# FFN gate and up by Strassen's method: seven quadrant products for eight, weight sums formed by accumulating DMAs

## The chip, the cores and the metric

One Trainium2 chip, one of its cores. The metric is the device time of one launch in microseconds (us); the kernel before takes 1047.01 us, the median of three runs (1046.59 to 1047.04). The rows and numbers of the trace come from one profiled execution with a span of 1045.3 us.

## What is computed

One decoder layer for 512 tokens, d_model 1024, float32: a half-step SwiGLU FFN, a mixing stage (a gated linear recurrence and a latent attention with a common input and output projection), a second half-step FFN, a per-layer embedding with a gate, and a final norm. The FFN, which the change is about, is

```python
def swiglu(x, w_gate, w_up, w_down):
    return (jax.nn.silu(x @ w_gate) * (x @ w_up)) @ w_down

h = h + 0.5 * swiglu(rms_norm(h, ln_ffn1[i]), w1_gate[i], w1_up[i], w1_down[i])   # D_FF = 2816
...
h = h + 0.5 * swiglu(rms_norm(h, ln_ffn2[i]), w2_gate[i], w2_up[i], w2_down[i])
```

## The kernel before

The residual `h` lies in SBUF as eight tiles of 128 features by 512 tokens (features on the partitions). All weights come from HBM as one stream of 128x128 blocks in the order of their use. `WStream.load` (L49) brings 16 blocks (1 MB) by one DMA of the SP queue into one of three raw tiles; `_split` (L68) turns eight blocks at a time into two float32r parts, `whi` by ScalarE (L70, a rounding copy) and `wlo` by VectorE (L71, raw minus high part). Of each part there are three tiles, and the splits run up to three pieces ahead of TensorE (`W.ahead`). Activations are split in the same way: `Norm.add` (L223) makes `xh` and `xl` of gain times `h` (L169, L170), and adds up the squares for the norm (L238, L239). The row factor of the norm, `rb`, is multiplied on after the product.

One block product is `mm3` (L157 to L161): three float32r matmuls, high by high, high by low, low by high, each of 128x128 stationary weights by 512 moving columns. Each matmul record has a weight-load record beside it.

`ffn` (L255) runs over 22 blocks of 128 hidden features. For each it makes the gate and the up product (`gu`, eight `mm3` each, one PSUM bank each, from the pools `acc` and `t` of three banks), and then the chain of L277 to L285: gate times `rb` (VectorE), Silu (ScalarE), times up (VectorE), and the split of the result into `ah` and `al`. After all 22 the `down` product runs (L291 to L298): eight blocks of 128 output features, 22 `mm3` each, times 0.5 and `rb`, added to `h`, and `next_norm.add`. In the first FFN three of the first products are taken k by k while `x` still arrives; after the fourth block `make_tables` (L302) makes the cosine and sine tables on VectorE, with two small DMAs of the POOL queue (L305, L336). In the output projection (L744 to L749) `n2.add` prepares the second FFN's input.

Within an engine the instructions stand in the order that a compile-time list scheduler chose: of the ready ones, the one that comes first in the program. So an engine is rarely held up by a waiting instruction that stands first in the text, but work that stands earlier in the text goes first wherever it is ready.

Of the kernel before, what the change touches and what calls it, by code (L numbers as in the profile page):

```python
# [29 lines left out]
RAW = 16  # L30

# columns of the packed vectors
# [5 lines left out]
class WStream:  # L38
    """The weights as one stream of 128x128 blocks in the order of their use, each split
    exactly into two float32r parts."""  # L40

    def __init__(self, nc, pool, dram, loads):
        self.nc, self.pool, self.dram = nc, pool, dram
        self.loads = list(loads)
        self.raws, self.ready, self.left = [], [], []
        self.n_load = self.n_piece = 0
        self.ahead = 1

    def load(self):  # L49
        start, n = self.loads.pop(0)  # L50
        t = self.pool.tile([P, RAW * P], F32, tag="wraw", name=f"wraw{self.n_load}", bufs=3)
        self.n_load += 1
        src = self.dram[start * P * P:(start + n) * P * P].rearrange("(p c) -> p c", p=P)
        self.nc.sync.dma_start(t[:, :n * P], src)
        self.raws += [(t, o, min(CH, n - o)) for o in range(0, n, CH)]

    def _piece(self):
        if not self.raws:
            self.load()
        raw, o, n = self.raws.pop(0)  # L60
        c = self.n_piece
        self.n_piece += 1
        hi = self.pool.tile([P, CH * P], F32R, tag="whi", name=f"whi{c}", bufs=3)
        lo = self.pool.tile([P, CH * P], F32R, tag="wlo", name=f"wlo{c}", bufs=3)
        self._split(raw, o, n, hi, lo)
        self.ready.append([(hi, lo, o, n) for o in range(n)])

    def _split(self, raw, o, n, hi, lo):  # L68
        src = raw[:, o * P:(o + n) * P]
        self.nc.scalar.activation(hi[:, :n * P], src, AF.Copy)  # L70
        self.nc.vector.tensor_tensor(lo[:, :n * P], src, hi[:, :n * P].bitcast(F32), op=ALU.subtract)  # L71

    def keep(self, new):
        """The next half of a piece in tiles of its own."""
        if not self.raws:
            self.load()
        raw, o, n = self.raws.pop(0)
        n_now = CH // 2
        if n > n_now:
            self.raws.insert(0, (raw, o + n_now, n - n_now))  # L80
        hi, lo = new("kh", F32R), new("kl", F32R)
        self._split(raw, o, n_now, hi, lo)
        return hi, lo

    def next(self, n=1):
        if not self.left:
            while len(self.ready) < self.ahead and (self.raws or self.loads):
                self._piece()
            self.left = self.ready.pop(0)
# [5 lines left out]


@with_exitstack
def block_kernel(ctx: ExitStack, tc: tile.TileContext, xT, pT, pos, wst, loads, vecs, lnf, cmask, tmask, out):
# [8 lines left out]
    W = WStream(nc, wpool, wst, loads)  # L107
# [27 lines left out]
    for k in range(KD):  # L135
        nc.sync.dma_start(h[k], xT[k * P:(k + 1) * P, :])
        if k < 4:
            W.load()
# [14 lines left out]

    def vcol(c):
# [8 lines left out]
    def split(src, hi, lo, g=None):  # L163
        """hi + lo = src * g, exactly."""
# [7 lines left out]
    def rsqrt_of(ss, n, width):  # L172
        """1 / sqrt(ss / width + eps) of a [P, n] view, by Newton's iteration."""
# [21 lines left out]
    def col_sums(sqs, out):  # L195
        """out[:, j] = sums over partitions (and over the tiles) of token block j."""
# [5 lines left out]
    def broadcast_ps(r):  # L202
        """[P tokens, 4 blocks] -> the same row of 512 tokens on every partition, in PSUM."""
# [13 lines left out]
    class Norm:  # L217
        """Splits g * h tile by tile, and gathers the sum of squares."""

        def __init__(self, gcol):  # L220
            self.gcol, self.hi, self.lo, self.sum = gcol, [], [], None

        def add(self, k, square=True):  # L223
            hi = tmp.tile([P, T], F32R, tag=f"xh{k}", name=nm("xh"), bufs=1)
            lo = tmp.tile([P, T], F32R, tag=f"xl{k}", name=nm("xl"), bufs=1)
            split(h[k], hi, lo, vcol(self.gcol + k))
            self.hi.append(hi)
            self.lo.append(lo)
# [11 lines left out]

        def finish(self):
# [6 lines left out]

    def row_bcast(r, tag):
# [5 lines left out]
    def ffn(norm, next_norm, first=(), extra=None):  # L255
        a_hi, a_lo = [], []
        first = list(first)

        def product(new):
            if first:  # L260
                return first.pop(0)
            u = new("gu")
            for k in range(KD):
                mm3(u, W.next(), norm.x(k), k == 0, k == KD - 1)
            return u

        waiting = []
        for f in range(KF):
            waiting.append((product(acc), product(tps)))
            if f == 0:  # L270
                r = norm.finish()
                continue
            if f == 1:
                rb = row_bcast(r, "rb")
            for g, u in waiting:
                gs = tmpt("gs")
                V.tensor_tensor(gs, g, rb, op=ALU.mult)  # L277
# [568 lines left out]
def _blocks(w1_gate, w1_up, w1_down, w_in, w_q_up, w_kv_up, w_out, w2_gate, w2_up, w2_down, w_ple_gate, w_ple_proj):  # L846
# [7 lines left out]
    def col(n):  # L854
        return slice(n, n + P)
# [92 lines left out]
```

## Time and profile before

| | |
|---|---|
| median of three runs | 1047.01 us |
| span of the profiled execution | 1045.3 us |
| TensorE busy in the span | 1034.2 us (99%), 4763 matmuls |
| VectorE / ScalarE busy | 519.2 us (50%) / 356.8 us (34%) |
| DMA | 97.48 MB, mean 93 GB/s |
| share of gate and up in the chain that ended last | 3 lines of 15% each |
| share of down in it | 3 lines of 8% each |

The page counts a matmul as busy from its start to its modelled end (389 ns here), and matmuls overlap; what one costs is read from the distance of the starts in the timeline. In a group of instructions the columns are: line, engine, operation, names and shapes, count | busy us, mean ns of one | idle time before them and what ended it.

### The profile page before, as it was taken

What the parts mean: (1) busy time and instruction counts of PE and PEld (TensorE: products, weight loads), DVE (VectorE), ACT (ScalarE), POOL (GpSimd) and SP (SyncE); (2) the same over time, 40 slices, a digit from 0 to 9 for tenths busy, and PEclk for the clock granted to TensorE, in tenths of its full rate; (3) what the DMA queues carried; (4) which work ended last, traced back from release to release, by engine and by line L of the source; (5) the groups of instructions that cost most, each with busy time, mean ns of one, the idle gap of its engine ahead of it and who ended that gap; (6) DMA issues with size and microseconds to landing.
All of it is one profiled execution on the core that took longest, in us unless ns stands there. A gap on an engine that the chain in (4) does not pass through costs nothing.

```text
span 1045.3 us, 11742 instructions
## 1 busy us (share of the span) xinstructions
PE 1034.2 (99%) x4763; PEld 845.5 (81%) x4763; DVE 519.2 (50%) x929; ACT 356.8 (34%) x567; POOL 2.5 (0%) x9
## 2 busy tenths in 40 slices
PE   9999999999999999999999999999999999999996
PEld 7888888888888888887666788888888888888885
DVE  7574433443343368775647655334443343344555
ACT  7333322233222232345444434322333232223332
POOL 0000000000000000000000000000000000000000
PEclk9999999999999999999999999999999999999998
DMA  7322323223232231212210232232232322323301
GB/s 285 116 102 82 119 81 109 93 84 118 81 104 98 83 119 42 71 61 91 91 41 1 81 103 98 81 114 88 85 117 80 118 84 87 116 81 126 116 22 60
DMA packets 16726, 97.48 MB, mean 93 GB/s; under 512 B 2096, under 2 KB 2352, under 8 KB 6048
## 3 DMA queue, kind: packets, MB, share of 16 engines
q1 hardware_dynamic: 16512, 96.24, 26.5%
q8 instruction: 37, 0.61, 0.2%
q0 software_dynamic: 160, 0.49, 0.2%
q14 instruction: 17, 0.14, 0.0%
HBM read 94.10 MB, written 2.10 MB: 92 GB/s over the span
## 4 chain that ended last, share of the span: by engine, by line
PE 97%; DMA 1%; DVE 1%; ACT 1%; issue 0%; SPq 0%; ACTq 0%; DVEq 0%
PE gu L160 15%; PE gu L159 15%; PE gu L161 15%; PE down L160 8%; PE down L159 8%; PE down L161 8%; PE ufq L159 2%; PE wo L159 1%; PE ufq L161 1%; PE ufq L160 1%; PE wo L160 1%; PE wo L161 1%; PE pg L159 1%; PE pg L161 1%; PE pg L160 1%; PE sl L536 1%
## 5 line engine op out<-in xcount | busy, mean ns | idle before, releaser
L70 ACT ACTIVATE whi<-wraw 128x1024 fp32r<-128x1024 f32 (+2 forms) x168 | 176.0, 1047 | 526.3 <-PE gu L160 187.2
L71 DVE TENSOR_TENSOR wlo<-wraw,whi 128x1024 fp32r<-128x1024 f32 (+2 forms) x168 | 203.0, 1208 | 150.0 <-ACT whi L70 148.4
L159 PE MATMUL gu<-xh,whi 128*128 128x512 f32 x704 | 274.4, 390 | 0.0
L161 PE MATMUL gu<-xh,wlo 128*128 128x512 f32 x704 | 274.0, 389 | 0.2 <-DVE wlo L71 0.2
L160 PE MATMUL gu<-xl,whi 128*128 128x512 f32 x704 | 273.8, 389 | 0.0
L159 PEld LDWEIGHTS gu<-xh,whi 128*128 128x128 f32 x704 | 132.3, 188 | 28.5 <-ACT whi L70 1.1
L161 PEld LDWEIGHTS gu<-xh,wlo 128*128 128x128 f32 x704 | 132.2, 188 | 28.1 <-DVE wlo L71 0.9
L160 PEld LDWEIGHTS gu<-xl,whi 128*128 128x128 f32 x704 | 132.2, 188 | 27.5
L159 PE MATMUL down<-ah,whi 128*128 128x512 f32 x352 | 136.9, 389 | 0.0
L160 PE MATMUL down<-al,whi 128*128 128x512 f32 x352 | 136.9, 389 | 0.0
L161 PE MATMUL down<-ah,wlo 128*128 128x512 f32 x352 | 136.9, 389 | 0.0
L282 DVE TENSOR_TENSOR a<-gu,gs 128x512 f32<-128x512 f32 x44 | 30.4, 691 | 128.3 <-PE gu L161 126.9
L277 DVE TENSOR_TENSOR gs<-gu,rb 128x512 f32<-128x512 f32 x44 | 30.3, 690 | 97.5 <-PE gu L161 97.3
L159 PEld LDWEIGHTS down<-ah,whi 128*128 128x128 f32 x352 | 66.1, 188 | 13.8
L161 PEld LDWEIGHTS down<-ah,wlo 128*128 128x128 f32 x352 | 66.1, 188 | 13.7
L160 PEld LDWEIGHTS down<-al,whi 128*128 128x128 f32 x352 | 66.1, 188 | 13.6
L169 ACT ACTIVATE xh<-h,vec 128x512 fp32r<-128x512 f32 x32 | 22.8, 718 | 27.9 <-DVE h L297 25.9
L167 DVE TENSOR_TENSOR al<-a,ah 128x512 fp32r<-128x512 f32 x44 | 30.1, 685 | 1.1 <-ACT ah L166 0.7
L166 ACT ACTIVATE ah<-a 128x512 fp32r<-128x512 f32 x44 | 27.8, 633 | 5.8 <-DVE a L282 5.8
L170 DVE SCALAR_TENSOR_TENSOR xl<-h,vec,xh 128x512 fp32r<-128x512 f32 x32 | 23.7, 747 | 9.5 <-ACT xh L169 9.5
L278 ACT ACTIVATE gs<-gs 128x512 f32<-128x512 f32 x44 | 27.2, 617 | 0.3
L159 PE MATMUL ufq<-xh,whi 128*128 128x512 f32 x64 | 26.2, 410 | 0.0
(256 smaller groups left out, 1092.7 us busy)
## 6 DMA issues: line engine op xcount, KB each, us to landing
wraw<-wst SPq DMA_DIRECT2D x83, 1024.0 KB, 4.9
h<-xT SPq DMA_DIRECT2D x8, 256.0 KB, 4.9
out<-y SPq DMA_DIRECT2D x8, 256.0 KB, 2.3
wraw<-wst SPq DMA_DIRECT2D x3, 384.0 KB, 5.4
wraw<-wst SPq DMA_DIRECT2D x2, 512.0 KB, 3.8
wraw<-wst SPq DMA_DIRECT2D x1, 768.0 KB, 4.2
rpb<-rpa SPq DMA_DIRECT2D x8, 64.0 KB, 2.0
praw<-pT SPq DMA_DIRECT2D x2, 256.0 KB, 4.0
```

The lines of the kernel that those rows point to most:

```text
L70: self.nc.scalar.activation(hi[:, :n * P], src, AF.Copy)
L71: self.nc.vector.tensor_tensor(lo[:, :n * P], src, hi[:, :n * P].bitcast(F32), op=ALU.subtract)
L159: PE.matmul(out, a[0], b[0], start=start, stop=False)
L160: PE.matmul(out, a[0], b[1], start=False, stop=False)
L161: PE.matmul(out, a[1], b[0], start=False, stop=stop)
L166: S.activation(hi, src, AF.Copy)
L167: V.tensor_tensor(lo, src, hi.bitcast(F32), op=ALU.subtract)
L169: S.activation(hi, src, AF.Copy, scale=g)
L170: V.scalar_tensor_tensor(lo, src, g, hi.bitcast(F32), op0=ALU.mult, op1=ALU.subtract)
L277: V.tensor_tensor(gs, g, rb, op=ALU.mult)
L278: S.activation(gs, gs, AF.Silu)
L282: V.tensor_tensor(a, u, gs, op=ALU.mult)
```

## The change

The gate and up products of hidden blocks 2 to 21 are made in ten pairs of blocks by Strassen's method in Winograd's form. The input is cut in four quadrants (two halves of 256 tokens by two halves of 512 features: A11, A12, A21, A22), the weights of a pair in four too (gate and up by two halves of the rows: B11, B12, B21, B22, eight 128x128 blocks each). Seven products of quadrants or sums of them take the place of eight: A11 B11, A12 B21, S1 T1, S2 T2, S3 T3, S4 B22, A22 T4. Each is 2 x 4 x 3 matmuls of 256 moving columns. Blocks 0 and 1 are still made in the old way.

- The sums S1 to S4 of the input are made once per FFN on VectorE and split (`Norm.forms`): in the first FFN after the input's splits, in the second within the output projection.
- The sums T1 to T4 of the weights are made in raw tiles: B12 is loaded, negated twice by ScalarE into the tiles N and Q, and DMAs of the POOL queue add quadrants from HBM onto them (`_add`): N + B11 is T1, then N + B22 is T2, Q + B22 is T3, and after one more negation by ScalarE N + B21 is T4, up to signs. All seven weight operands of a pair are split as before.
- Partial results are read from PSUM in between by ScalarE and VectorE (`start_pair`, `end_pair`), the next pair's first two products stand between this pair's.
- `down` runs in two halves: over blocks 0 to 11 after the fifth pair, over 12 to 21 at the end; both add to `h`.
- Loads are 8 blocks (0.5 MB) now, into seven raw tiles; the scratch space for descriptors shrinks to 2048 bytes. The first FFN starts with four products k by k, not three.

```diff
-RAW = 16
+NRAW = 7
+HT = T // 2
+MO = [0, 4, 1, 5, 2, 6, 3, 7]
...
+    def load(self, start, n):
+        t = self.raw()
+        self.nc.sync.dma_start(t[:, :n * P], self.source(start, n))
+        return t
...
+    def _add(self, t, g, name):
+        self.nc.gpsimd.dma_start(out=t, in_=self.source(GROUPS[g][name], CH), accum_op=ALU.add)
+
+    def _begin(self, g):
+        if g not in GROUPS or g in self.groups:
+            return
+        S = self.nc.scalar
+        d = self.groups[g] = {"N": self.load(GROUPS[g]["B12"], CH), "Q": self.raw()}
+        S.activation(d["Q"], d["N"], AF.Copy, scale=-1.0)
+        S.activation(d["N"], d["N"], AF.Copy, scale=-1.0)
+        self._add(d["N"], g, "B11")
+        self._add(d["Q"], g, "B22")
+
+    def _form(self, g, what):
+        self._begin(g)
+        d = self.groups[g]
+        if what in ("T1", "T2", "T4"):
+            return d["N"]
+        return d["Q"] if what == "T3" else self.load(GROUPS[g][what], CH)
+
+    def _formed(self, g, what):
+        d = self.groups[g]
+        if what == "T1":
+            self._add(d["N"], g, "B22")
+        elif what == "B11":
+            self._begin(g + 1)
+        elif what == "T3":
+            self.nc.scalar.activation(d["N"], d["N"], AF.Copy, scale=-1.0)
+            self._add(d["N"], g, "B21")
...
+        def forms(self, k):
+            left, right = slice(0, HT), slice(HT, T)
+            c, c2 = self.gcol + k, self.gcol + k + 4
+            a21 = tmpt("a21", tag="sq", bufs=2)[:, :HT]
+            f = tmp.tile([P, 4, HT], F32, tag="at", name=nm("sf"), bufs=1)
+            S.activation(a21, h[k][:, right], AF.Copy, scale=vcol(c))
+            V.scalar_tensor_tensor(f[:, 0], h[k + 4][:, right], vneg[:, c2:c2 + 1], a21, op0=ALU.mult, op1=ALU.subtract)
+            V.scalar_tensor_tensor(f[:, 1], h[k][:, left], vneg[:, c:c + 1], f[:, 0], op0=ALU.mult, op1=ALU.subtract)
+            V.scalar_tensor_tensor(f[:, 2], h[k][:, left], vcol(c), a21, op0=ALU.mult, op1=ALU.subtract)
+            V.scalar_tensor_tensor(f[:, 3], h[k + 4][:, left], vcol(c2), f[:, 1], op0=ALU.mult, op1=ALU.subtract)
+            for i in range(4):
+                t = slot("sx", F32R).rearrange("p (two t) -> p two t", two=2)
+                split(f[:, i], t[:, 0], t[:, 1])
+                self.s[k, i + 1] = t
...
+        def product(bank, what, begin=False, end=False):
+            hi, lo = W.form()
+            for i in range(2):
+                o = bank[:, i * HT:(i + 1) * HT]
+                for k in range(4):
+                    c = slice((2 * k + i) * P, (2 * k + i + 1) * P)
+                    x = norm.operand(what, k)
+                    PE.matmul(o, hi[:, c], x[:, 0], start=begin and i == 0 and k == 0, stop=False, skip_group_check=True)
+                    PE.matmul(o, hi[:, c], x[:, 1], start=False, stop=False, skip_group_check=True)
+                    PE.matmul(o, lo[:, c], x[:, 0], start=False, stop=end and i == 1 and k == 3, skip_group_check=True)
...
+        def start_pair(d):
+            d["c"] = tps("c")
+            product(d["c"], "S1", begin=True)
+            yield
+            d["a"] = acc("a")
+            product(d["a"], "A11", begin=True)
+            d["m1"] = tmpt("m1")
+            S.activation(d["m1"], d["a"], AF.Copy)
+            yield
+
+        def end_pair(f, d, between):
+            b = tps("b")
+            product(b, "A12", begin=True, end=True)
+            gs1 = tmpt("gs")
+            V.tensor_tensor(gs1, b, d["m1"], op=ALU.add)
+            V.tensor_tensor(by_half(gs1), by_half(gs1), r_of(0), op=ALU.mult)
+            S.activation(gs1, gs1, AF.Silu)
+            product(d["a"], "S2")
+            u2 = slot("u2")
+            S.activation(u2, d["a"], AF.Copy)
+            next(between, None)
+            product(d["a"], "S3")
+            u3 = slot("u3")
+            S.activation(u3, d["a"], AF.Copy)
+            V.tensor_tensor(u3, d["c"], u3, op=ALU.add)
+            next(between, None)
+            product(d["c"], "S4", end=True)
+            V.tensor_tensor(u2, d["c"], u2, op=ALU.add)
+            product(d["a"], "A22", end=True)
+            at = tmp.tile([P, 2, T], F32, tag="at", name=nm("at"), bufs=1)
+            V.tensor_tensor(at[:, 0], u2, gs1, op=ALU.mult)
+            gs2 = tmpt("gs")
+            V.tensor_tensor(by_half(gs2), by_half(d["a"]), r_of(1), op=ALU.mult)
+            S.activation(gs2, gs2, AF.Silu)
+            V.tensor_tensor(at[:, 1], u3, gs2, op=ALU.mult)
+            for i in range(2):
+                gated(f + i, at[:, :, i * HT:(i + 1) * HT])
...
+        second = down(range(12, KF), True)
+        for f in range(2, KF, 2):
+            d_next = {}
+            end_pair(f, d, start_pair(d_next) if f + 2 < KF else second)
+            d = d_next
+            if f == 10:
+                for _ in down(range(12), False):
+                    pass
+        for _ in second:
+            pass
...
-    first = [acc("gu"), tps("gu"), acc("gu")]
-    for k in range(KD):
+    first = [acc("gu"), tps("gu"), acc("gu"), tps("gu")]
+    for k in MO:
         n1.add(k, square=False)
         for u in first:
-            mm3(u, W.next(), n1.x(k), k == 0, k == KD - 1)
+            mm3(u, W.next(), n1.x(k), k == MO[0], k == MO[-1])
+    for k in range(4):
+        n1.forms(k)
...
+        for p in range(PAIRS):
+            forms(p, "B21", "T2")
+            forms(p + 1, "T1")
...
+            forms(p, "T3")
+            forms(p + 1, "B11")
...
+            forms(p, "B22", "T4")
+            if p == 4:
+                down(range(12))
```

## Rows read from the trace of the kernel before

**Rows 1.** The page: its head, the engines' busy time, the chain's shares by engine.
```profile
span 1045.3 us, 11742 instructions
PE 1034.2 (99%) x4763; PEld 845.5 (81%) x4763; DVE 519.2 (50%) x929; ACT 356.8 (34%) x567; POOL 2.5 (0%) x9
...
PE 97%; DMA 1%; DVE 1%; ACT 1%; issue 0%; SPq 0%; ACTq 0%; DVEq 0%
```

**Rows 2.** Timeline, gate and up, 30 matmuls apart: start us, us, engine, line, tile.
```profile
643.44 0.39 PE L161 MATMUL gu<-xh,wlo 128*128 128x512 f32 x1
...
650.24 0.39 PE L161 MATMUL gu<-xh,wlo 128*128 128x512 f32 x1
```

**Rows 3.** Timeline, mixing stage: 448 columns (12 apart) and 512 columns (10 apart).
```profile
440.15 0.36 PE L161 MATMUL uc<-whi,xl 128*128 128x448 f32 x1
...
442.59 0.36 PE L161 MATMUL uc<-whi,xl 128*128 128x448 f32 x1
...
394.25 0.39 PE L159 MATMUL ufq<-xh,whi 128*128 128x512 f32 x1
...
396.55 0.39 PE L160 MATMUL ufq<-xl,whi 128*128 128x512 f32 x1
```

**Rows 4.** Chain of work in order of time: start us, us, piece; plain float32 matmuls.
```profile
498.58 0.43 PE sc L569 x2
...
545.70 2.23 PE oh L715 x20
```

**Rows 5.** Groups by line, shapes apart: VectorE and ScalarE instructions.
```profile
L71 DVE TENSOR_TENSOR wlo<-wraw,whi 128x1024 fp32r<-128x1024 f32 x162 | 198.3, 1224 | 149.5 <-ACT whi L70 147.9
L282 DVE TENSOR_TENSOR a<-gu,gs 128x512 f32<-128x512 f32 x44 | 30.4, 691 | 128.3 <-PE gu L161 126.9 <-ACT gs L278 1.4
L170 DVE SCALAR_TENSOR_TENSOR xl<-h,vec,xh 128x512 fp32r<-128x512 f32 x32 | 23.7, 747 | 9.5 <-ACT xh L169 9.5
L405 DVE TENSOR_TENSOR qe<-ufq,rb 128x256 f32<-128x256 f32 x8 | 3.1, 416 | 5.3 <-PE ufq L161 5.3
L70 ACT ACTIVATE whi<-wraw 128x1024 fp32r<-128x1024 f32 x162 | 171.8, 1060 | 525.2 <-PE gu L160 187.2 <-issue 151.0 <-PE down L160 126.6
L166 ACT ACTIVATE ah<-a 128x512 fp32r<-128x512 f32 x44 | 27.8, 633 | 5.8 <-DVE a L282 5.8
L252 ACT ACTIVATE rb<-rbp 128x512 f32<-128x512 f32 x3 | 1.7, 580 | 0.0
```

**Rows 6.** Windows: stretch, us, busy us of the engines, clock, DMA share, GB/s.
```profile
0.00:25.00 25.00, 23.27 (x92) 17.68 (x93) 17.52 (x34) 18.93 (x29) 1.38 (x7) 1.00 0.82 298
...
100.00:200.00 100.00, 100.00 (x443) 82.80 (x442) 40.60 (x46) 29.59 (x37) 0.00 (x0) 1.00 0.27 95
...
570.00:628.00 58.00, 57.98 (x267) 47.00 (x265) 33.20 (x47) 24.06 (x37) 0.00 (x0) 1.00 0.26 89
```

**Rows 7.** DMA issues: size of one, median us from issue to landing.
```profile
wraw<-wst SPq DMA_DIRECT2D x83, 1024.0 KB, 4.9
...
wraw<-wst SPq DMA_DIRECT2D x2, 512.0 KB, 3.8
...
posi<-pos POOLq DMA_DIRECT2D x1, 256.0 KB, 3.7
```

**Rows 8.** Timeline of the first FFN: VectorE's and TensorE's start, the tables on VectorE.
```profile
4.87 0.75 DVE L170 SCALAR_TENSOR_TENSOR xl<-h,vec,xh 128x512 fp32r<-128x512 f32 x1 [1.86 <-ACT xh L169]
...
5.30 0.97 PE L159 MATMUL gu<-xh,whi 128*128 128x512 f32 x2
...
54.99 0.42 DVE L307 CAST ang<-posi 128x512 f32<-128x512 int32 x1
...
64.02 0.42 DVE L326 TENSOR_SCALAR kr<-kr 128x512 f32<-128x512 f32 x1
```

More of the change, by code (lines that the diff above doesn't have):

```diff
@@ L52, in load, with raw, source @@
+    def raw(self):
+        t = self.pool.tile([P, CH * P], F32, tag="wraw", name=f"wraw{self.n_load}", bufs=NRAW)
         self.n_load += 1
[L53 to L60, printed above, removed]
+        return t
+    def source(self, start, n):
+        return self.dram[start * P * P:(start + n) * P * P].rearrange("(p c) -> p c", p=P)
@@ L62, in _piece @@
         self.n_piece += 1
[L63 to L71, printed above, removed]
@@ L73, in keep, with _plain @@
-    def keep(self, new):
[L75 to L80, printed above, removed]
+        return (self.pool.tile([P, CH * P], F32R, tag="whi", name=f"whi{c}", bufs=3),
+                self.pool.tile([P, CH * P], F32R, tag="wlo", name=f"wlo{c}", bufs=3))
+    def _plain(self, start, n):
+        t = self.raws.pop(0) if self.raws else self.load(start, n)
+        hi, lo = self._pair()
+        self._split(t[:, :n * P], hi[:, :n * P], lo[:, :n * P])
+        return [(hi, lo, o, n) for o in range(n)]
@@ new lines, in _piece @@
+    def _piece(self):
+        kind, x, n = self.items.pop(0)
+        if kind == "p":
+            self.ready.append(self._plain(x, n))
+        else:
+            t = self._form(x, n)
+            hi, lo = self._pair()
+            self._split(t, hi, lo)
+            self._formed(x, n)
+            self.ready.append([(hi, lo, o, CH) for o in range(CH)])
+    def keep(self, new):
+        assert not self.left and not self.ready
+        if self.half is None:
+            _, start, n = self.items.pop(0)
+            t = self.load(start, n)
+            src, self.half = t[:, :CH // 2 * P], t[:, CH // 2 * P:]
+        else:
+            src, self.half = self.half, None
@@ L94, in next, with form, block_kernel @@
         return hi[:, s], lo[:, s]
+    def form(self):
+        assert not self.left
+        self._fill()
+        hi, lo, _, _ = self.ready.pop(0)[0]
+        return hi, lo
 @with_exitstack
-def block_kernel(ctx: ExitStack, tc: tile.TileContext, xT, pT, pos, wst, loads, vecs, lnf, cmask, tmask, out):
+def block_kernel(ctx: ExitStack, tc: tile.TileContext, xT, pT, pos, wst, items, vecs, lnf, cmask, tmask, out):
     nc = tc.nc
@@ L134, in block_kernel @@
     nc.sync.dma_start(vec, vecs)
-    for k in range(KD):
+    for i, k in enumerate(MO):
         nc.sync.dma_start(h[k], xT[k * P:(k + 1) * P, :])
-        if k < 4:
-            W.load()
+        if i < 4:
+            W.early()
     ones = const.tile([P, 1], F32, name="ones")
@@ L743, in block_kernel @@
     n2 = Norm(V_LN2)
-    for m in range(KD):
+    for m in MO:
         u = acc("wo")
```

250 lines of the change are left out of this document (146 added, 104 removed).

## Prediction

> **What bounds the kernel now.** I read the page first: TensorE is busy 99% of the span and carries 97% of the chain that ended last [rows 1]. So a microsecond less on TensorE is a microsecond less in the end, as long as no other engine comes in between. What a matmul costs isn't its 0.39 us record, since records overlap; it is the distance of two starts. In gate and up 30 matmuls of 512 columns stand 6.80 us apart, 226.7 ns each [rows 2]. At the granted clock of 1.00, which is 2.4 GHz [rows 6], 512 columns alone are 213.3 ns, so 13.3 ns come on top. The windows then say what lies idle: in a stretch of pure gate and up VectorE works 40.6 of 100 us, ScalarE 29.6, the DMA engines 0.27 of the time at 95 GB/s [rows 6]. The change trades TensorE's columns for work on these three. All sums are made against the profiled execution, 1045.3 us [rows 1], plus the 1.7 us by which the median of the runs (1047.0) lies above that span.
>
> **TensorE, per pair.** Before, a pair of blocks is 2 x 2 products x 8 `mm3` x 3 = 96 matmuls of 512 columns: 96 x 226.7 ns = 21.76 us. After, 7 products x 24 = 168 matmuls of 256 columns. No row shows a float32r matmul of 256 columns, so its price t is bounded. Low end: plain float32 (`oh`, 128 columns) holds the array for 256 cycles an instruction too and has its own 128x128 weight load: 20 in 2.23 us, 111.5 ns [rows 4]. High end: the line through 512 columns in gate and up (226.7) and 448 columns in the mixing stage (12 in 2.44 us, 203.3 ns [rows 3]) falls by 0.366 ns a column and gives 133 ns at 256. But 512 columns cost 230 ns in that stage too (10 in 2.30 us [rows 3]), 3.3 more than in gate and up; without these the 448 columns cost 200.0, which is 186.7 for the columns and again 13.3. The extra seems fixed per matmul, so I take t = 106.7 + 13.3 = 120 ns: 168 x 120 = 20.16 us, 1.60 less per pair, 32.0 for the 20 pairs of both FFNs. The ends: at 111.5 the pair is 18.73, 60.6 less in all; at 133 it is 22.3, 12 more in all. Break-even is 129.5 ns. The whole change hangs on this price: an eighth of the columns is saved, and the fixed part is paid 168 times instead of 96.
>
> The Trainium skill ("TensorE: Matmul & The Clock Gate", section "Back-to-back issue gap") gives columns by 2.4 plus 2.5 ns. By it 256 columns are 109.2 ns, the pair 18.3 us and the saving 68 us. The float32 rows agree (512 cycles in 215 ns, `sc` [rows 4]); the float32r rows do not (226.7 where the rule says 215.8 [rows 2]).
>
> **VectorE and ScalarE, per pair.** VectorE: seven low parts for four, 7 x 1.224 = 8.6 us, and nine passes over 512 columns (two for gate's left half, two adds, gate's right half, two products, two low parts), 9 x 0.691 = 6.2: 14.8 of 20.2 us [rows 5]. ScalarE: seven high parts and three negations of the same size, 10 x 1.060, three copies from PSUM at 0.580 and four more at 0.633: 14.9 [rows 5]. Both fit at 73%. A split (2.3 us for both parts) is released two products, 5.8 us, before its use, so 3.5 us are spare. New waits of TensorE: S3 overwrites a bank that ScalarE must have copied within the one product between (2.88 us): 0.58 plus a 1.06 us split in front, hidden. S4 waits for a copy and an add, 0.58 + 0.69, with a split in front of each, 1.06 + 1.22: 3.55 at worst against 2.88. That is 0 to 0.7 us a pair; I take 0.2, 4 us in all, since splits often aren't in front.
>
> **DMA, per pair.** 95 GB/s at a share of 0.27 [rows 6] is 352 GB/s of all 16 engines, so 0.5 MB cost 1.49 us of them. Four plain loads are 6.0 us. No row shows an accumulating transfer: at the least it costs as a plain one, 1.49; if reading the source, reading the tile and writing it go one after the other, 4.47. I take two passes, 2.98, reads and writes being two directions: the pair then takes 17.9 of 20.2 us, hidden. Landing: 0.5 MB took 3.8 us on SP, 0.25 MB on POOL 3.7 [rows 7]; doubled, some 7 us as an estimate. The tightest sum is T4's: negated and issued after T3's split, due three products later, 8.6 us; the others have five or six. So these are hidden; past 8.6 + 3.5 us each further microsecond comes back once a pair, behind it on ScalarE the copies that TensorE waits for.
> The Trainium skill ("DMA: Bandwidth & Descriptors", section "Rules for kernel authors") says that an accumulate reads its destination and writes it later. No run here shows that yet.
>
> **First FFN's start.** VectorE begins at 4.87 us [rows 8]. Before S1 it must do eight low parts of x (8 x 0.747 = 6.0), the plain pieces (2 x 0.69 + 3 x 1.224 = 5.1), the forms (32 passes over 256 columns x 0.416 = 13.3) and T1's low part (1.2): 25.6 us [rows 5], so 30.5 without a pause, 35.3 if the seven sums of squares (0.69 each), earlier in the text, come first. TensorE begins at 5.30 [rows 8] and is through with 96 plain matmuls at 27.1, say 28 with a slow start. Hole: 2.5 to 7.3; I take 6. The tables follow, from 54.99 to 64.44 us in one block on VectorE [rows 8]; before, an idle VectorE hid them. Now VectorE is behind, they stand earlier in the text than the pairs' low parts, and 3.5 us are spare: a hole of about 6, from 0 to 9.5. POOL's two table transfers wait for these same tiles in front of the first additions; counted here. Together 12, from 3 to 22 (the plain blocks' chain and the norm's factor on top).
>
> **The rest.** Second FFN: the forms' 13.3 us go into a stage where VectorE is busy 33.2 of 58 [rows 6], and 96 plain matmuls (21.8 us) stand before S1: 0; uncovered, 7 as in the first. Ends of the FFNs: after the last A22 three products and two splits, 0.69 + 0.63 + 0.69 + 0.63 + 0.69 = 3.3 us [rows 5], stand before blocks 20 and 21 of `down`, most of whose first column has been used up between the products: 0 to 3.3 each, I take 2, 4 in all. After the fifth pair 30 matmuls (6.8 us) stand before block 10: 0. `down` keeps its matmuls; its second evacuation is 1.4 us a column on VectorE beside 6.8 of TensorE: 0. The early load of Sigmoid's table goes; ScalarE has room: 0.
>
> Sum: 1047.0 - 32.0 + 4 + 12 + 4 = 1035 us.
>
> **Rivals.**
> Full rate: the weight load hides as in the float32 rows, t = 111.5. For it: the same cycles and the same load. Against: float32r pays 13.3 over its columns, float32 2 to 5. 1047 - 60.6 + 20 = 1006. Chance 0.14. By the Trainium skill's gap rule above it would be 1047 - 68 + 20 = 999; only a part of this chance would go there.
> The DMA engines bind (slower): an addition costs more than (20.2 - 6.0) / 4 = 3.55 us of the engines; at 3.95 the pair is as long as before, at 4.47 it is 23.8 us. Then nothing is saved, and the holes of 16 us stay: 1063 at 3.95, 1047 + 41 + 16 = 1104 at 4.47; the middle is 1084. For it: 17.9 of 20.2 us is a share of 0.89 for 400 us; the highest window of before is 0.82, at the start [rows 6]. Against: two passes fit. Chance 0.22.
> The price of 256 columns lies on the line, 133 ns: 1047 + 12 + 20 = 1079. Against: the 230 ns beside it. Chance 0.10.
> VectorE and ScalarE don't keep up: start 22, ends 7, 0.7 a pair 14: 1047 - 32 + 43 = 1058 at full size, and halfway to the forecast's holes of 20 it is 1047, no change. Chance 0.12.
>
> **How the numbers follow.** The forecast has 0.42, with a range of its own of 1020 to 1046 (t from 116 to 124, start 3 to 22). A measurement tells 0.2%, 2.1 us, from no change. Faster: 0.38 of the forecast's 0.42 and full rate's 0.14, 0.52. Same: 0.03 and 0.02 of the last rival, 0.05. Slower: 0.01, 0.22, 0.10 and 0.10, 0.43. Cases of both signs hold much of the chance, so the range is wide: down to full rate, 1006 (0.07 below it), up to just above the DMA rival's middle, 1088 (0.11 above).
>
> **What would show it.** Starts of the pair's matmuls 120 ns apart (111 or 133 for the rivals); TensorE's idle time before `c`, `a`, `b` named by `whi` or `wlo` behind an addition (DMA), by the copies of `u2` and `u3` (PSUM), or hardly there; the additions' landing under 12 us and a DMA share under 0.9 in the pairs; two holes before 65 us with VectorE busy through them. I am wrong if 256 columns cost over 129 ns, or if an addition takes the engines over 3.55 us.

## The result, and the profile after

The changed kernel takes 1114.8 us (median of four runs, 1110.6 to 1116.3) beside 1046.9 of the kernel before on the same chip: the ratio is 1.064, 95% interval 1.063 to 1.065. It is slower by 6.4%, where 1035 was forecast, and the forecast's range ended at 1088. The page of its profiled run, head, DMA queues, chain, two groups of matmuls and the landings of the two kinds of transfer:

```profile
span 1114.5 us, 15580 instructions
PE 1043.0 (94%) x6203; PEld 921.0 (83%) x6203; DVE 668.5 (60%) x1147; ACT 518.0 (46%) x786; POOL 72.2 (6%) x89
...
q1 hardware_dynamic: 28752, 96.25, 25.7%
q0 software_dynamic: 11680, 42.44, 21.2%
...
PE 71%; DMA 12%; issue 6%; DVE 6%; ACT 4%; POOL 0%; SPq 0%; ACTq 0%; POOLq 0%; DVEq 0%
...
L382 PE MATMUL a<-x,whi 128*128 128x256 f32 x320 | 93.2, 291 | 32.2 <-ACT u L415 26.1
L382 PE MATMUL c<-sx,whi 128*128 128x256 f32 x320 | 105.7, 330 | 15.4 <-DVE u L416 13.3
...
wraw<-wst SPq DMA_DIRECT2D x169, 512.0 KB, 3.6
wraw<-wst POOLq DMA_DIRECT2D x80, 512.0 KB, 6.1
```

Against [rows 1] TensorE's share of the chain fell from 97% to 71%, and transfers hold 12% of it. TensorE's idle time stands before `a` and `c`, put down to the copy of `u3` (line 415, ScalarE) and the addition after it (line 416, VectorE). One pair shows how. A prime marks a product of the next pair (A11'). The windows first (stretch, us, busy us of the engines, granted clock, DMA share, GB/s): a full product, then the product behind the hole, then two long stretches of pairs.

```profile
263.00:269.00 6.00, 6.00 (x51) 5.90 (x50) 3.55 (x5) 2.78 (x4) 0.00 (x0) 1.00 0.57 169
...
288.70:293.80 5.10, 5.10 (x24) 5.10 (x25) 1.07 (x1) 1.06 (x1) 0.00 (x0) 0.50 0.47 180
260.00:350.00 90.00, 78.53 (x589) 77.23 (x588) 49.09 (x56) 46.11 (x58) 10.46 (x12) 0.91 0.65 156
700.00:819.00 119.00, 107.28 (x819) 105.28 (x819) 69.73 (x81) 66.17 (x83) 14.50 (x17) 0.93 0.71 173
```

The same pair in the timeline (start us, us, engine, line, tile; in brackets idle time and what ended it): TensorE, ScalarE, VectorE (the split of T3), the loads' queue, the additions' queue.

```profile
281.13 0.28 PE L384 MATMUL a<-sx,wlo 128*128 128x256 f32 x1
...
284.01 0.28 PE L384 MATMUL a<-x,wlo 128*128 128x256 f32 x1
287.13 0.38 PE L382 MATMUL a<-x,whi 128*128 128x256 f32 x1 [2.83 <-ACT u L415]
288.69 0.58 PE L382 MATMUL c<-sx,whi 128*128 128x256 f32 x1 [1.18 <-DVE u L416]
...
293.98 0.41 PE L383 MATMUL a<-x,whi 128*128 128x256 f32 x1
...
276.43 1.05 ACT L73 ACTIVATE whi<-wraw 128x1024 fp32r<-128x1024 f32 x1
284.59 2.00 ACT L73 ACTIVATE whi<-wraw 128x1024 fp32r<-128x1024 f32 x2 [7.11 <-DMA wraw<-wst]
286.50 0.58 ACT L415 ACTIVATE u<-a 128x512 f32<-128x512 f32 x1
...
274.77 1.22 DVE L74 TENSOR_TENSOR wlo<-wraw,whi 128x1024 fp32r<-128x1024 f32 x1
...
276.02 0.33 SPq L63 DMA_DIRECT2D wraw<-wst  x1
...
269.18 0.87 POOL L89 DMA_DIRECT2D wraw<-wst  x1 [15.76 <-ACT wraw L97]
271.07 0.86 POOL L89 DMA_DIRECT2D wraw<-wst  x1 [1.02 <-ACT wraw L98]
273.28 1.75 POOL L89 DMA_DIRECT2D wraw<-wst  x2 [1.35 <-DVE wlo L74]
```

Read it backwards. TensorE ends A11' at 284.1 and stands until `u3` is copied out of bank `a`. S3, whose result the copy takes, was over at 281.2, but ScalarE has two splits queued ahead of the copy, those of B22 and of T4, and waits 7.11 us for a transfer there. The copy starts at 286.50, five microseconds late. The section on the kernel before says that an engine is rarely held up by a waiting instruction; here the fixed order holds ScalarE up in front of work that was ready. Then S4 waits 1.18 us for the addition. After this standstill its 24 matmuls take 5.29 us for 2.88 (288.69 to 293.98): the granted clock is 0.50, the 1.2 GHz level, where it was 1.00 before.

The first matmul after the hole writes `a`: it is A22's, and it stands ahead of S4, where the program's text has it behind. So T4 is due one product earlier than the program's text says.

What ScalarE waits for is B22's load. The loads' queue sends it at 276.02 only, because it takes over the tile that T3 leaves: the low part of T3's split, the last to read that tile, ends at 275.99. The waits of that queue from 263 to 276.5 (us, times, longest):

```profile
SPq L63 <- DVE wlo L74: 13.3, 2, 12.2
```

And then the load does not run. The DMA queues in two stretches behind its issue (packets, MB, and the time of their packets as a share of 16 engines' time; packets overlap, so a share can pass 100%), and the time to landing of this one load:

```profile
q0 software_dynamic: 198, 0.70, 105.8%
...
q0 software_dynamic: 82, 0.33, 67.7%
q1 hardware_dynamic: 80, 0.33, 35.5%
...
wraw<-wst SPq DMA_DIRECT2D x1, 512.0 KB, 8.5
```

From 276 to 279.5 us (first line) only the additions' queue moves packets: four additions were issued between 269.2 and 273.9, and three of them are still under way. The load's first packet moves 3.6 us after its issue; for the 81 loads of this trace that were issued with no other load or addition under way it was 1.0 us (median). From 280 to 282.5 both queues move, packet for packet, an addition's packet taking nearly twice as long. The load lands after 8.5 us, where the median of all loads is 3.6. T4's addition, the last of the four, took 10.4 us and lands 0.2 us before it, so both splits ahead of the copy wait.

Where the time went, summed over the starts of all neighbouring matmuls of the FFNs (what a distance exceeds 120 ns, or 227 ns in `down`; up to 0.26 us of excess counted as half clock, that is, as matmuls at the 1.2 GHz level, more as standstill), in us:

| stretch | standstill | half clock | predicted |
|---|---|---|---|
| first FFN, up to the second pair's A12 (75.8 us) | 16.9 | 4.0 | 12 |
| first FFN, pairs from there | 30.6 | 17.1 | 2, and 2 at the end |
| second FFN, up to the first A12 | 3.2 | 0.2 | 0 |
| second FFN, pairs from there | 19.5 | 11.3 | 2, and 2 at the end |

Together 102.8 for 20. With TensorE's own 32 us less this is +70.8; the two spans differ by 69.2.

### The profile page after: what moved, and what is told of

It reads as the page before. It is cut to its first block, busy times and chain, and to the rows that moved or that the text cites. A ratio compares the mean times of both kernels' runs of the same rounds, so it can differ in the third digit from the quotient of the medians.

```text
span 1114.5 us, 15580 instructions
## 1 busy us (share of the span) xinstructions
PE 1043.0 (94%) x6203; PEld 921.0 (83%) x6203; DVE 668.5 (60%) x1147; ACT 518.0 (46%) x786; POOL 72.2 (6%) x89
## 4 chain that ended last, share of the span: by engine, by line
PE 71%; DMA 12%; issue 6%; DVE 6%; ACT 4%; POOL 0%; SPq 0%; ACTq 0%; POOLq 0%; DVEq 0%
DMA wraw<-wst 11%; PE down L230 7%; PE down L231 7%; PE down L232 7%; DVE wlo L74 3%; PE c L382 3%; PE a L384 3%; PE a L383 3%; PE a L382 3%; ACT whi L73 3%; PE c L383 2%; PE c L384 2%; PE ufq L230 1%; PE b L382 1%; PE b L383 1%
## 5 line engine op out<-in xcount | busy, mean ns | idle before, releaser
L73 ACT ACTIVATE whi<-wraw 128x1024 fp32r<-128x1024 f32 (+1 forms) x229 | 237.5, 1042 | 381.4 <-DMA wraw<-wst 93.9
L74 DVE TENSOR_TENSOR wlo<-wraw,whi 128x1024 fp32r<-128x1024 f32 (+1 forms) x229 | 275.0, 1206 | 206.5 <-ACT whi L73 205.1
L382 PE MATMUL a<-x,whi 128*128 128x256 f32 x320 | 93.2, 291 | 32.2 <-ACT u L415 26.1
L382 PE MATMUL c<-sx,whi 128*128 128x256 f32 x320 | 105.7, 330 | 15.4 <-DVE u L416 13.3
L384 PE MATMUL c<-sx,wlo 128*128 128x256 f32 x320 | 102.4, 320 | 0.0
L383 PE MATMUL c<-sx,whi 128*128 128x256 f32 x320 | 102.4, 320 | 0.0
L382 PE MATMUL a<-sx,whi 128*128 128x256 f32 x320 | 91.6, 286 | 5.1 <-ACT m L399 4.6
L384 PE MATMUL a<-sx,wlo 128*128 128x256 f32 x320 | 91.3, 285 | 0.3 <-DVE wlo L74 0.3
L384 PE MATMUL a<-x,wlo 128*128 128x256 f32 x320 | 91.0, 284 | 0.5 <-DVE wlo L74 0.5
L383 PE MATMUL a<-x,whi 128*128 128x256 f32 x320 | 91.1, 285 | 0.0
L383 PE MATMUL a<-sx,whi 128*128 128x256 f32 x320 | 91.1, 285 | 0.0
L382 PEld LDWEIGHTS c<-sx,whi 128*128 128x128 f32 x320 | 73.9, 231 | 19.7 <-DVE u L416 16.2
L383 PEld LDWEIGHTS c<-sx,whi 128*128 128x128 f32 x320 | 74.3, 232 | 0.0
L384 PEld LDWEIGHTS c<-sx,wlo 128*128 128x128 f32 x320 | 73.9, 231 | 0.3 <-DVE wlo L74 0.3
```

The source lines that it names most:

```text
L73: self.nc.scalar.activation(hi, src, AF.Copy)
L74: self.nc.vector.tensor_tensor(lo, src, hi.bitcast(F32), op=ALU.subtract)
L382: PE.matmul(o, hi[:, c], x[:, 0], start=begin and i == 0 and k == 0, stop=False, skip_group_check=True)
L383: PE.matmul(o, hi[:, c], x[:, 1], start=False, stop=False, skip_group_check=True)
L384: PE.matmul(o, lo[:, c], x[:, 0], start=False, stop=end and i == 1 and k == 3, skip_group_check=True)
```

## The experiments

**Are the transfers the cause at all?**

```diff
     def _add(self, t, g, name):
-        self.nc.gpsimd.dma_start(out=t, in_=self.source(GROUPS[g][name], CH), accum_op=ALU.add)
+        pass
```

> All 80 accumulating transfers are left out (the weight sums are then not formed, so this run shows only time); every other instruction stays. Theory A: in each pair TensorE stands still before block row A22/S4 because u3's copy out of PSUM is queued on ScalarE behind the splits of B22 and T4, and these wait for transfers that land late; the following product then runs at half clock. By A the holes (2.3 to 4 us) and the slow product (2.3 us) of nearly all pairs go, the start's some 20 us stay: about 1035 (1025 to 1050), clock of the pairs 0.98 or more. Rival B, VectorE and ScalarE have too much work for a pair of 20 us: nothing but DMA work was taken away, so the pairs stay at 25 us and the time above 1095. Rival C, PSUM is copied too late because the copies themselves are long: as B.

Measured: 1034.9 us, 0.989 (0.987 to 0.990). A stretch of pairs in its windows:

```profile
216.00:302.00 86.00, 86.00 (x714) 85.61 (x713) 59.41 (x69) 54.40 (x68) 0.00 (x0) 1.00 0.34 102
```

TensorE is busy for all of it at full clock, with the same work on VectorE (69% of the time) and ScalarE (63%). Rivals B and C fall: neither engine is the bound, and the copies themselves are not too long.

**Which transfer, and through which queue?** Two changes, each alone and both.

```diff
-NRAW = 7
+NRAW = 8
```

> Only change: eight buffers for raw weights for seven, so that B22's load no longer waits for T3's split to free one. Theory A: B22's load leaves several us earlier and ahead of the queued additions, but T4's split, which waits for its addition (landing 10 to 11 us after its issue), still stands in front of u3's copy: holes about 1 us shorter, 1095 (1080 to 1105). Rival A1, the late buffer is the whole cause: holes gone, about 1040. Rival B, too much work on VectorE and ScalarE: unchanged, 1110 to 1117.

```diff
-            S.activation(u3, d["a"], AF.Copy)
+            copy = S.activation(u3, d["a"], AF.Copy)
             V.tensor_tensor(u3, d["c"], u3, op=ALU.add)
-            next(between, None)
+            with tc.issue_after(copy.ins):
+                next(between, None)
```

> Only change: an issue order that puts u3's copy on ScalarE ahead of T4's split. Theory A: the copy still stands behind B22's split, whose load lands as late as T4's addition (284.5 and 284.3 us in the pair at 270 us): holes about 1 us shorter, 1095 (1080 to 1105). Rival A2, T4's late addition is the whole cause: holes gone, about 1040. Rival B: unchanged, 1110 to 1117.

> Both changes: eight raw buffers and u3's copy ahead of T4's split. Theory A: neither late transfer stands in front of the copy any more; the holes of the pairs and the half clock behind them go, the first FFN's start stays: about 1040 (1030 to 1060), more than the two single changes together. Rival A1 or A2: the same time as the one single change that already did it. Rival B: above 1095. Rival D, TensorE then waits for T4 itself, because its addition lands 10 us after its issue and is due 9 us after: holes of 1 to 3 us before A22, 1065 to 1085.

Measured: the eighth buffer alone 1051.9 us (1.005, 1.003 to 1.006), the order alone 1110.3 (1.062, 1.058 to 1.066), both 1042.9 (0.997, 0.996 to 0.999). Both single runs missed their expected 1080 to 1105, on opposite sides. The buffer is nearly the whole cure, 62.8 of the 71.8 us that both bring. With the order alone the copy still stands behind B22's split, and its late load is enough to hold it: in the pair at 263 us ScalarE waits 8.14 us in front of that split alone. The loads' queue and the landing of B22's load with the eighth buffer, ScalarE in two pairs, and two stretches of pairs:

```profile
250.52 13.15 SPq L63 DMA_DIRECT2D wraw<-wst  x4
...
wraw<-wst SPq DMA_DIRECT2D x1, 512.0 KB, 5.0
...
260.99 1.06 ACT L73 ACTIVATE whi<-wraw 128x1024 fp32r<-128x1024 f32 x1 [1.39 <-issue]
263.87 1.06 ACT L73 ACTIVATE whi<-wraw 128x1024 fp32r<-128x1024 f32 x1 [1.82 <-PE a L383]
264.84 0.58 ACT L415 ACTIVATE u<-a 128x512 f32<-128x512 f32 x1
...
114.76 1.06 ACT L73 ACTIVATE whi<-wraw 128x1024 fp32r<-128x1024 f32 x1 [6.01 <-DMA wraw<-wst]
...
90.00:178.00 88.00, 84.23 (x629) 81.32 (x629) 54.60 (x63) 49.77 (x62) 10.46 (x12) 0.96 0.76 194
232.00:320.00 88.00, 88.00 (x725) 87.29 (x724) 60.23 (x70) 56.09 (x71) 12.20 (x14) 1.00 0.77 188
```

In the pair at 252 us B22's load leaves 13 us before S3 ends instead of 5, lands in 5.0 us, and the copy follows S3's end by 1.1 us. T4's split still stands ahead of it, released by TensorE and no longer by a transfer. Theory A held that T4's late addition would keep the copy waiting just as long; but the eighth buffer moves the additions too. The first of the burst goes out 4.1 us before the pair's first A12 matmul instead of 0.6, and T4's lands 9.2 us after that matmul instead of 14.6, ahead of S3's end at 11.5. So this run does not part the load from the addition. In the second stretch TensorE has no gap although the DMA share rose from 0.65 to 0.77: the engines were never full on average. In the first stretch one hole is left. There ScalarE waits 6.01 us in front of T4's split, whose addition landed at 114.7 us: a late T4 alone can hold the copy as well. The order of the copy takes this hole out; that is some 6 of the 9 us between 1051.9 and 1042.9, and the rest are gaps under 0.8 us and slow matmuls in the second FFN.

**Why was the load late?**

```diff
-        self.nc.gpsimd.dma_start(out=t, in_=self.source(GROUPS[g][name], CH), accum_op=ALU.add)
+        self.nc.gpsimd.dma_start(out=t, in_=self.source(GROUPS[g][name], CH))
```

> The changed kernel with seven buffers, its 80 additions replaced by plain transfers of the same bytes on the same queue at the same places (the weight sums are then not formed). It parts the price of the addition itself (2.95 us of the engines) from the number of transfers. Theory: B22's load is late because it leaves at T3's split and stands behind four additions, 12 us of the engines within 5; as plain ones these are 6 us, the load lands about 4 us after its issue instead of 8.5, in time for u3's copy: 1035 to 1045, as without them. Rival: the number of transfers or their queue is what delays the load: holes stay at half size or more, 1075 to 1110.

Measured: 1052.0 us (1.005, 1.004 to 1.007). Its queue of the same 80 transfers, their landing, and a stretch of pairs:

```profile
q0 software_dynamic: 11680, 42.44, 11.8%
...
wraw<-wst POOLq DMA_DIRECT2D x80, 512.0 KB, 4.1
...
225.00:310.00 85.00, 81.45 (x671) 80.55 (x671) 54.84 (x62) 49.79 (x63) 6.86 (x13) 1.00 0.58 185
```

A share of 0.118 of 1050.7 us, by 80, is 1.55 us of all engines for a plain transfer; 0.212 of 1114.5, by 80, is 2.95 for an addition. Standstill and half clock together are 38.3 us here, 102.8 with additions and 20.4 without any: 18 us hang on the transfers as such, 64 on their being additions. The theory has the larger part, not the whole; the expected 1035 to 1045 was too low, and the rival's 1075 to 1110 too high.

```diff
-        elif what == "T3":
+        elif what == "T2":
             self.nc.scalar.activation(d["N"], d["N"], AF.Copy, scale=-1.0)
             self._add(d["N"], g, "B21")
```

> The changed kernel with its seven buffers; only T4's negation and addition move from behind T3's split to behind T2's, one product (2.9 us) earlier. The prediction had called T4's addition the tightest transfer. Theory, by the run with eight buffers: B22's late load is the cause, T4's addition only a neighbour in the burst that it stands behind; the burst then ends 1 to 3 us earlier, B22's load lands by as much earlier, and the holes shrink but stay: about 1080 (1060 to 1100). Rival, the prediction's step: T4's landing alone is what delays u3's copy: holes gone, 1040 to 1050.

Measured: 1109.0 us (1.058, 1.057 to 1.060). ScalarE in the pair at 267 us, behind T3's split:

```profile
282.23 2.00 ACT L73 ACTIVATE whi<-wraw 128x1024 fp32r<-128x1024 f32 x2 [7.40 <-DMA wraw<-wst]
```

The expectation was too low and the rival fell. Counted from the pair's first A12 matmul, T4's addition now lands at 11.4 us for 14.6, but B22's load at 14.7 as before: it still leaves at T3's split, behind the same four additions. ScalarE waits as long as ever. So the addition that the prediction called the tightest is not the cause alone: the late load is enough to hold the copy. Nor is that addition harmless, as the hole at 114 us with the eighth buffer shows. How much the load alone would give back, with T4's addition as late as it was, no run parts.

**Is the half clock a price of its own?**

```diff
+            idle = aux("idle")
+            for _ in range(24):
+                tc.keep_in_program_order(PE.matmul(idle[:, :HT], ones_r, norm.xs[0][:, 0, :HT], start=True, stop=True))
             product(d["c"], "S4", end=True)
```

> The changed kernel, all as it was, with 24 matmuls of 256 columns into an unused bank behind A11' in each pair (2.88 us at full clock), where TensorE stood still for 2 to 5 us. Question: is the slow product behind the hole (24 matmuls in some 5.1 us for 2.9) a price of its own of the standstill, and how large. Theory: the clock falls because TensorE stood still; with the hole filled, what is left of it is under 2 us and the product runs at 120 ns a matmul. About 26 of the 32 us that matmuls at half clock cost in the changed kernel go, none of the 70 us of holes: 1114.8 - 26 = about 1089 (1080 to 1100), clock above 0.98 in the pairs. Rival: the slow product has another cause (its weights or operands come late, matmul by matmul): the fill changes nothing, or costs up to 57 us where there is no hole: 1110 to 1140.

Measured: 1112.3 us (1.063, 1.061 to 1.065). TensorE in two pairs, and a stretch of them:

```profile
257.60 3.00 PE L420 MATMUL idle<-x,ones_r 128*128 128x256 f32 x24
260.44 0.28 PE L382 MATMUL c<-sx,whi 128*128 128x256 f32 x1
...
263.31 0.28 PE L382 MATMUL a<-x,whi 128*128 128x256 f32 x1
...
310.25 0.39 PE L382 MATMUL c<-sx,whi 128*128 128x256 f32 x1 [2.68 <-DVE u L416]
...
243.00:341.00 98.00, 94.56 (x770) 93.72 (x769) 54.49 (x62) 50.55 (x63) 11.26 (x13) 0.98 0.66 162
```

The cause of the slow product is shown, and it is the standstill: behind a filled gap S4's 24 matmuls take 2.87 us (260.44 to 263.31), and the time lost to the half clock falls from 32.6 to 10.7 us. The gain expected from that, 26 us, isn't there. The fill itself is 20 x 2.88 = 57.6 us, the standstill that it took away only 38 (70.2 to 32.2): pairs that had no hole pay it in full, and some still wait (2.68 us at 310.25). The time lies in the rival's range, for its second reason, the cost of the fill, and not for its first. So the price of the clock can't be added to that of the hole as if TensorE alone set the pace.

**What is left: the first FFN's start.** From here on with the eighth buffer and the copy's order. First the rotary tables, moved beside the first half of `down`:

```diff
-        if extra:
-            extra()
         second = down(range(12, KF), True)
...
             if f == 10:
+                if extra:
+                    extra()
                 for _ in down(range(12), False):
```

> Eight buffers, u3's copy ahead of T4's split, and the rotary tables moved from the first pair to the first half of down, where VectorE has room. The prediction counted 6 us for them (0 to 9.5). Theory: the hole of 3.1 us and the slow product behind it at 72 to 80 us go: 1042.9 - 6 = 1037 (1034 to 1040). Rival: additions that land late hold that place anyway: 1041 to 1043.

Measured: 1034.9 us (0.988, 0.987 to 0.990), 8 less than 1042.9, as expected and a little more. The waits of TensorE from 28 to 82 us, in the changed kernel, name what stood there (us, times, longest); the first line is the tables' block on VectorE, with 3.1 us in the kernel that this one is compared with and no line here:

```profile
PE b L382 <- DVE u L419: 4.7, 1, 4.7
PE a L382 <- ACT m L399: 3.3, 1, 3.3
PE a L382 <- ACT whi L73: 2.7, 1, 2.7
PE c L382 <- ACT whi L73: 1.7, 1, 1.7
```

The other three stand behind additions: the split of T1 (ScalarE waits 3.00 us for a transfer before it, up to 28.48 us), behind that and 2.2 us of forms and squares the split of B11, and behind T2's split (5.46 us, up to 43.74) the copy of `m1`. Two runs change the order of the additions' queue. N's addition goes ahead of Q's, in the first run for all pairs, in the second (with one more `if`) for the first pair of each FFN; in both, the second pair's two additions go behind T2's of the first pair:

```diff
-        self._add(d["N"], g, "B11")
-        self._add(d["Q"], g, "B22")
+        add = self._add(d["N"], g, "B11")
+        with self.tc.issue_after(add.ins):
+            self._add(d["Q"], g, "B22")
...
-        elif what == "B11":
+        elif what == ("T2" if g % PAIRS == 0 else "B11"):
             self._begin(g + 1)
```

> As the kernel with the tables moved, and two changes of order in the additions' queue: N's first addition ahead of Q's, and the second pair's two first additions behind T2's of the first pair in each FFN. Theory: at the first FFN's start TensorE waits at 28 to 47 us for T1's and T2's additions, which stand second and fifth in that queue and land at 29.7 and 45.0, not for VectorE as the prediction had it; by this order they land at about 27 and 41, and 5 to 8 us of holes and half clock go: 1037 - 6 = 1031 (1027 to 1034). Rival, VectorE holds the start (the forms, the sums of squares): unchanged, 1036 to 1038.

> As the kernel with the tables moved; the two changes of order in the additions' queue (N before Q, the second pair's additions behind T2's) for the first pair of each FFN alone. Theory: the order for all pairs gained 3.5 us at the first FFN's start and lost some 4 us in the later pairs, where Q's addition came second and T3's split after it; for the first pair alone the gain stays and the loss goes: 1034.9 - 3.5 = 1031.4 (1030 to 1033). Rival: the start's gain is given back by the next wait there (the norm's factor): 1034 to 1036.

Measured: 1037.1 us (0.991, 0.989 to 0.993) for all pairs, 1031.6 (0.985, 0.983 to 0.987) for the first alone. The first missed: it is 2.2 us slower than the 1034.9 that it is compared with, in its rival's range. The rival's reason does not hold, though: with the order everywhere the second pair's A12 starts 3.4 us earlier, but the later pairs lose 5.1 us to standstill and half clock where they lost 0.9. With it in the first pair alone 3.3 us stay, as expected. So additions do hold a part of the start.

Last, on the kernel with the tables moved and without these orders, more plain work ahead of the first pair, and then the norm's factor taken earlier:

```diff
+        if plain == 4:
+            first += [whole(acc("gu")), whole(tps("gu"))]
+            r = norm.finish()
+            rb = row_bcast(r, "rb")
+            for f in range(2):
+                plain_out(f, first[2 * f], first[2 * f + 1])
+            first += [whole(acc("gu")), whole(tps("gu"))]
+            for f in range(2, 4):
+                plain_out(f, first[2 * f], first[2 * f + 1])
...
-PAIRS = KF // 2 - 1
+PAIRS = (KF // 2 - 2, KF // 2 - 1)
```

> As the kernel with the tables moved, but the first FFN computes four blocks with eight products per pair before its pairs begin (nine pairs for ten), and the sums of squares stand ahead of the forms in the text. Theory: the start's holes and half clock (14 us from 29 to 73 us, and the slower products round them) are a chain of load, negation, addition, split and forms that has nothing to hide behind; 21.8 us of plain products hide it: 14 less, 1.6 more for the pair that is not saved: 1034.9 - 12 = 1023 (1019 to 1028). Rival: VectorE's work (forms and sums) or the norm's factor holds the start wherever the pairs begin: 1032 to 1038.

```diff
-            first += [whole(acc("gu")), whole(tps("gu"))]
-            r = norm.finish()
+            r = norm.r
+            first.append(whole(acc("gu")))
             rb = row_bcast(r, "rb")
+            first.append(whole(tps("gu")))
...
+    n1.r = n1.finish()
     for k in range(4):
         n1.forms(k)
```

> As the kernel with four plain blocks, but the norm's factor is taken directly behind the sums of squares, and its spread over the partitions between the two products of the third block, instead of behind both. Theory: what was left at the first FFN's start, TensorE idle from 39.1 to 47.4 us but for three small products and 2.6 us of half clock behind it, is the norm's factor alone; the fourth block's banks are released by it. It then runs beside the third block: 1029.0 - 8 - 2.6 = about 1018.5 (1016 to 1022). Rival: the sums of squares or the forms hold the factor up on VectorE until after the third block: 1025 to 1029.

Measured: 1029.0 us (0.983, 0.981 to 0.984), then 1024.0 (0.978, 0.976 to 0.979). The first missed its range by 1 us: the pairs then start without a hole, but the fourth plain block waits for its banks, from 39.1 to 47.4 us, for the norm's factor. The second missed by 2 us: the factor still comes behind the third block, but TensorE stands there for 3.5 us instead of 7.4. The page of this fastest kernel, the starts of A12 in two pairs that follow each other, and a stretch of pairs:

```profile
span 1022.8 us, 15375 instructions
PE 1006.7 (98%) x6131; PEld 887.6 (87%) x6131; DVE 664.6 (65%) x1141; ACT 513.4 (50%) x777; POOL 68.3 (7%) x85
...
228.31 0.28 PE L382 MATMUL b<-x,whi 128*128 128x256 f32 x1
...
248.47 0.28 PE L382 MATMUL b<-x,whi 128*128 128x256 f32 x1
...
62.00:142.00 80.00, 80.00 (x669) 80.00 (x668) 53.38 (x60) 52.18 (x64) 12.67 (x15) 1.00 0.85 209
```

A pair is 20.16 us, to the hundredth what was predicted. In the stretch from 62 to 142 us TensorE has no gap either, with the DMA engines busy 0.85 of the time. So the method is worth its 1.6 us a pair here; the changed kernel had lost that and more to transfers that came late.

## Why the prediction was wrong

**TensorE, per pair: right.** 256 columns start 120 ns apart at full clock (2.88 us a product), the value taken between 111.5 and 133, and the pair is 20.16 us. The rivals at full rate and at 133 ns fall.
The gap rule of the Trainium skill ("TensorE: Matmul & The Clock Gate", section "Back-to-back issue gap"), which that section gives for isolated matmuls and by which 256 columns are 109.2 ns, does not hold for these matmuls: the trace has 120.

**VectorE and ScalarE: right.** 69% and 63% busy in the stretch without holes, for 73% by the sum.

**DMA, per pair: the sum was right, the conclusion was not.** This is the step that failed. An addition costs 2.95 us of the engines, for 2.98 taken from two passes; a plain transfer 1.55, for 1.49. That two passes are the reason is not shown: the number fits, and it was picked from between 1.49 and 4.47. The threshold of 3.55 us was not reached, and the pairs can run at a share of 0.77 to 0.85. But "So these are hidden" was concluded from that mean and from landings taken one at a time, and put at nothing in the sum; the pairs lost 78.5 us to standstill and half clock.
The rule that the prediction quoted from the Trainium skill ("DMA: Bandwidth & Descriptors", section "Rules for kernel authors"), that an accumulate reads its destination and writes it later, fits a price of 1.9 times a plain transfer's; the order of reading and writing no run here shows.

Three things were left out. Plain loads were taken to leave whenever wanted: seven tiles, of which a pair and the next hold several for long, let B22's load go only at T3's split. The eighth tile gave back 62.8 us, by this load and by earlier additions. Four additions go out within 5 us and need 12 us of the engines, so whatever is issued behind them lands late: 8.5 us for a plain load priced at 3.8, 10.4 us for T4's addition, estimated at 7. And the slack was counted to the product that uses the weights; but the splits stand ahead of `u3`'s copy on ScalarE, which is due when S3 ends. For T4's addition in the pair shown that is 7.3 us behind its issue, where the prediction gave it 8.6 + 3.5.

The signs that the prediction named for itself did not catch this: the additions landed under 12 us (78 of 80), the share stayed under 0.9, and neither 129 ns nor 3.55 us was passed. None of them looked at a plain load or at the engine whose queue a transfer stops.

The Trainium skill says ("DMA: Bandwidth & Descriptors", section "Queues, rings and completion order") that each DMA engine takes turns between the queues that have work, packet by packet. The trace agrees for 280 to 282.5 us (82 packets to 80). For 276 to 279.5, where the load had been issued and only additions moved, it does not show such turns: about 1 us of this every load waits for its first packet, and whether the rest is the engines' order or a late start of the load's own work stays open.

**PSUM waits: the place was named, the price was not.** 0 to 0.7 us a pair were computed for the wait of S4, with splits in front of the copy costed by their duration. A split in front that waits for a transfer costs what the transfer costs: 2.83 + 1.18 us in the pair shown. The sentence that past its slack "each further microsecond comes back once a pair, behind it on ScalarE the copies that TensorE waits for" described the mechanism, for T4; it got no rival and no chance. TensorE's idle time was named by the copy of `u3`, which the prediction had listed as the sign of these PSUM waits.

**The clock: not in the prediction.** Behind each such hole of the pairs 12 to 26 matmuls ran at the 1.2 GHz level, 1.4 to 2.7 us more (2.4 in the pair shown); 32.6 us in all.

**First FFN's start: 21 us for 12**, inside the 3 to 22 that were given, but that is partly luck. The tables' hole was there (4.7 us and a slow product; moving them gave 8). The rest was put on VectorE's forms; the waits name weights behind additions, and the two last runs the norm's factor. How much of it the forms held was not tried by itself.

**Ends of the FFNs and the second FFN's forms:** 4 us were counted for the ends; `down` follows the last pair without a gap, 0. The second FFN lost 3.4 us up to its first A12, where 0 was taken.

**The rivals.** The slower one, DMA engines bind, was right in sign and in the word DMA, but its condition (over 3.55 us an addition) did not hold: it would have shown a share near 1, and the pairs had 0.65 to 0.71. The measured time lies above the range because none of the cases joined a late transfer to an engine's queue that stands still behind it.

## What to carry over

A transfer is hidden when it lands in time, and that is not read from the mean share of the engines: list what is issued in one burst, sum its engine time, and put each landing behind what was issued before it; ask of every load which tile it waits for. Then follow an in-order engine's queue behind each wait to the first instruction that TensorE needs, since that one has the shortest slack. One more buffer and one fixed order made a change that lost 6.4% gain 0.3% (0.1 to 0.4), and with the tables moved and the start filled it gains 2.2%.

## What the runs showed of the hardware

An accumulating transfer of 512 KB takes 2.95 us of the 16 DMA engines and lands in 6.1 us (median of 80) where a plain one on the same queue takes 1.55 and lands in 4.1; issued as the last of four within 5 us it took 10.4 us. A plain load on another queue, issued behind such a burst, had no packet moved for its first 3.6 us (1.0 with nothing else under way) and then shared packet for packet. After 2.83 and 1.18 us of standstill with one matmul between them the granted clock was 0.50 for the next 24 matmuls; 1.43 and 1.18 us, in the second FFN, were enough for a mean of 0.61, while gaps of 1.3 and 1.6 us that lay 5 us apart, before that FFN's first A12 matmul at 702.3 us, were followed, from the third matmul on, by starts 0.12 us apart. The window of the second case, columns as above:

```profile
737.40:741.80 4.40, 4.40 (x24) 4.40 (x25) 1.04 (x1) 0.82 (x1) 0.00 (x0) 0.61 0.59 182
```

With the gap filled by matmuls into an unused bank the clock was 0.98 over a stretch of 98 us.
